# A two-layer decoder trunk on one core: x turned without its norm, the norm's factor applied behind the projections, and all attention products on 128 rows and columns

## The chip, the cores and the metric

The kernel runs on one core of a Trainium2 chip. The metric is the device time of one execution in microseconds (us), lower is better. A core has a matrix engine (TensorE, PE in the rows; PEld is its weight load), a vector engine (VectorE, DVE), a scalar engine (ScalarE, ACT) and a fourth one, GpSimd (POOL), each with its own queue that it works through in order, and queues that issue transfers (SP is the one that only does that).

## The reference, cut to what matters

```python
def rms_norm(x, g):
    y = xf * lax.rsqrt(jnp.mean(xf * xf, axis=-1, keepdims=True) + EPS)
    return (y * g.astype(jnp.float32)).astype(x.dtype)
...
    for layer in range(DEPTH):                      # DEPTH 2, x is (1, 256, 1024)
        h = rms_norm(x, norm1_g[layer])
        proj = h @ w_in[layer]
        dq, dk, dv, fq, fk, fv, ff, ga, gb = jnp.split(proj, split_points, axis=-1)
        y_diff = diff_attention(...)                # 4 heads, 2 maps of 64 each, values of 128
        y_fox = forgetting_attention(...)           # 8 heads of 64, decay from log_sigmoid(ff + b)
        merged = jax.nn.sigmoid(ga) * (y_diff @ w_diff_o[layer]) + jax.nn.sigmoid(gb) * (y_fox @ w_fox_o[layer])
        x = x + merged @ w_out[layer]
        x = x + peer_ffn(rms_norm(x, norm2_g[layer]), ...)
    return rms_norm(x, final_norm_g)

def peer_ffn(h, w_query, sub_keys, expert_u, expert_v):
    q = (t @ w_query).reshape(T, PEER_HEADS, 2, PEER_HALF)      # 8 heads
    s = jnp.einsum('thpd,pnd->thpn', q, sub_keys)
    top_s, top_i = lax.top_k(s, PEER_TOPK)                      # 16 of 128, twice; then 16 of 256
...
    gates = jax.nn.softmax(best_s, axis=-1)
...
        act = jax.nn.gelu(jnp.einsum('td,ted->te', tb, expert_u[eb]).astype(jnp.float32), approximate=False)
        return jnp.einsum('te,ted->td', (gb * act).astype(tb.dtype), expert_v[eb])   # 16384 experts
```

## The kernel before

Tokens are 256, in two halves tt of 128; the width of 1024 is eight pieces k of 128. Every large matrix product runs three times in a reduced float32 form: each operand is split into a high part (ScalarE copies it, line 92 for weights) and a low part (VectorE subtracts, line 93), and hi x hi, hi x lo and lo x hi are summed. Weights come as 656 blocks of 128 x 1024 in one fixed order (plan): per layer 8 for V and the forget gate, 32 for queries, keys and gates (wA), 8 and 8 for the output products, 16 for the expert queries (wQ), 128 for expert_u and 128 for expert_v. There are three raw buffers, filled from SP's queue, and three pairs hi and lo. A call of weights for block n first emits the splits up to block n + 2, so that the split of block n + 2 stands in ScalarE's and VectorE's queues ahead of all that is written after it, and can begin when TensorE is done with block n - 1.

The order is written by hand (manual_schedule): an instruction stands in its engine's queue where the Python code emits it, and generators such as forget, diff_head, fox_pair and select are advanced between projections by next, so that their pieces fall between the matmuls.

Per layer: norm_t makes the normalised, turned activations hT (the sums of squares on ScalarE, the root on GpSimd and VectorE, then 16 products of x with a diagonal matrix on TensorE, line 248, which norm and turn at once, then high and low parts, lines 253 and 254). mixer runs the V product (eight blocks, tokens on the rows), the projections wA with the attention heads between them, and the output products; sum_b adds the last product up, its last two blocks piece by piece in four pieces of 128 x 512, so that each piece of x is finished early. peer then has its own norm_t, 16 query projections, 48 projections of expert_u while select picks the experts on VectorE (each projection gives it 1.35 us of work, PIECE_US), then the rest of expert_u with the dense gate matrices (one_hots, dense, apply), and the sum over expert_v, again by sum_b.

## Time and profile before

| | |
|---|---|
| median of 3 runs | 2009.3 us (2009.29 to 2009.52) |
| the profiled execution | 2009.3 us, its span 2007.5 us |
| TensorE busy | 1992.8 us, 14042 matmul passes |
| VectorE, ScalarE busy | 1412.1 us, 1058.8 us |
| GpSimd busy | 27.4 us |

A busy matmul overlaps the next, so TensorE's busy time tells only that it hardly ever has nothing to do. The chain of waits is the better view: it follows the work that ended last back to what released it, and gives a matmul the time until the next one goes on. The hand-overs between the stages are the places to look at: where sum_b ends and the next projections begin.

### The profile page before, as it was taken

To read this page: it belongs to the slowest core of one execution; us is meant where nothing else is said; L and a number is where in the kernel's file an instruction comes from. 1 tells how busy PE (TensorE), PEld (TensorE's weight loads), DVE (VectorE), ACT (ScalarE), POOL (GpSimd) and SP (SyncE) were. 2 spreads that over 40 slices of the span, in tenths; PEclk is the share of its full clock that TensorE was granted. 3 is DMA by queue.
4 is the path that set the end of the run, shared out by engine and by line. 5 is a ranking of instruction groups with operands and counts; after the bars stand their busy time and mean duration, and the time that the engine had idled before them with its cause. 6 is when DMAs were issued, how large, how long until landed. Compare 5 with 4: busy or idle time off the path is not lost.

```text
span 2007.5 us, 35728 instructions
## 1 busy us (share of the span) xinstructions
PE 1992.8 (99%) x14042; PEld 1833.4 (91%) x14042; DVE 1412.1 (70%) x2867; ACT 1058.8 (53%) x1954; POOL 27.4 (1%) x49
## 2 busy tenths in 40 slices
PE   9999999999999999999999999999999999999998
PEld 8998999999999888888899989999999998888886
DVE  5667798788888555555566677987888885555555
ACT  6665556554444444444466655465444444444444
POOL 2000000000000000000010000000000000000000
PEclk9999999999999999999999999999999999999999
DMA  6445555555555555555554455565555555555554
GB/s 226 149 157 168 161 180 181 187 164 163 158 168 167 190 189 189 189 189 189 189 167 148 148 180 159 190 180 179 167 159 161 167 174 188 189 189 189 189 188 153
DMA packets 97451, 351.96 MB, mean 175 GB/s; under 512 B 11473, under 2 KB 11510, under 8 KB 97281
## 3 DMA queue, kind: packets, MB, share of 16 engines
q1 hardware_dynamic: 95040, 345.09, 54.5%
q0 software_dynamic: 1664, 3.53, 0.6%
q8 instruction: 110, 1.80, 0.4%
q10 hardware_dynamic: 576, 1.05, 0.1%
q14 instruction: 61, 0.49, 0.1%
HBM read 348.56 MB, written 1.71 MB: 174 GB/s over the span
## 4 chain that ended last, share of the span: by engine, by line
PE 99%; DVE 0%; DMA 0%; issue 0%; ACT 0%; POOL 0%; SPq 0%; ACTq 0%; DVEq 0%
PE acc L154 39%; PE ps L121 17%; PE ps L122 17%; PE ps L123 17%; PE acc L760 3%; PE ps L154 1%; PE acc L783 1%; PE acc L248 1%; PE acc L627 1%; PE ps L557 0%; PE acc L569 0%; PE acc L644 0%; DMA x<-x 0%; PE acc L122 0%; PE acc L123 0%
## 5 line engine op out<-in xcount | busy, mean ns | idle before, releaser
L93 DVE TENSOR_TENSOR lo<-raw,hi 128x1024 fp32r<-128x1024 f32 (+1 forms) x656 | 801.7, 1224 | 500.2 <-ACT hi L92 498.2
L92 ACT ACTIVATE hi<-raw 128x1024 fp32r<-128x1024 f32 (+1 forms) x656 | 694.4, 1059 | 396.3 <-PE acc L154 389.2
L121 PE MATMUL ps<-hT,hi 128*128 128x256 f32 x2784 | 794.6, 285 | 0.0
L122 PE MATMUL ps<-hT,hi 128*128 128x256 f32 x2784 | 784.6, 282 | 0.0
L123 PE MATMUL ps<-hT,lo 128*128 128x256 f32 x2784 | 778.9, 280 | 0.0
L154 PE MATMUL acc<-hi,cut 128*128 128x512 f32 x2048 | 561.1, 395 | 0.0
L121 PEld LDWEIGHTS ps<-hT,hi 128*128 128x128 f32 x2784 | 523.0, 188 | 3.9 <-issue 3.7
L123 PEld LDWEIGHTS ps<-hT,lo 128*128 128x128 f32 x2784 | 524.9, 189 | 0.0
L122 PEld LDWEIGHTS ps<-hT,hi 128*128 128x128 f32 x2784 | 523.4, 188 | 0.3
L154 PEld LDWEIGHTS acc<-hi,cut 128*128 128x128 f32 x2048 | 385.4, 188 | 90.0
L154 PE MATMUL acc<-lo,cut 128*128 128x512 f32 x1024 | 321.9, 394 | 0.0
L154 PEld LDWEIGHTS acc<-lo,cut 128*128 128x128 f32 x1024 | 192.4, 188 | 45.8
L730 ACT ACTIVATE g<-ps 128x8 f32<-128x8 f32 (+31 forms) x158 | 44.5, 282 | 265.3 <-PE ps L123 260.7
L675 ACT ACTIVATE bufa<-ps 128x256 f32<-128x256 f32 x96 | 36.9, 384 | 115.5 <-PE ps L123 115.5
L751 DVE TENSOR_TENSOR ohG<-oh,tT 128x2048 f16<-128x2048 f16 x64 | 78.4, 1225 | 2.2
L749 DVE TENSOR_TENSOR oh<-iotax,tT 128x2048 f16<-128x2048 f16 x64 | 77.8, 1216 | 0.0
L760 PE MATMUL acc<-ohG,oh 128*128 128x128 f16 x1024 | 70.0, 219 | 0.0
L701 DVE TENSOR_TENSOR cut<-bufb,cut 128x256 fp32r<-128x256 f32 x160 | 67.1, 419 | 0.0
L700 ACT ACTIVATE cut<-bufb 128x256 fp32r<-128x256 f32 x160 | 64.0, 400 | 0.0
L760 PEld LDWEIGHTS <-oh 128*128 128x128 f16 x1024 | 58.9, 97 | 2.9
L734 DVE TENSOR_TENSOR bufb<-bufb,g 128x8 f32<-128x8 f32 (+31 forms) x158 | 46.1, 292 | 15.3 <-ACT g L730 15.3
L772 DVE SCALAR_TENSOR_TENSOR bufa<-acc,bufa 128x192 f32<-128x192 f32 x128 | 44.8, 350 | 0.0
(231 smaller groups left out, 1383.9 us busy)
## 6 DMA issues: line engine op xcount, KB each, us to landing
raw<-uT SPq DMA_DIRECT2D x256, 512.0 KB, 3.7
raw<-expert_v SPq DMA_DIRECT2D x256, 512.0 KB, 3.6
raw<-wA SPq DMA_DIRECT2D x64, 512.0 KB, 3.6
raw<-wQ SPq DMA_DIRECT2D x32, 512.0 KB, 3.6
raw<-wV SPq DMA_DIRECT2D x16, 516.0 KB, 4.0
raw<-wO SPq DMA_DIRECT2D x16, 512.0 KB, 3.6
raw<-w_out SPq DMA_DIRECT2D x16, 512.0 KB, 4.4
tb<-table POOLq DMA_DIRECT2D x2, 640.0 KB, 6.1
```

Of the source, the lines that this page charges most:

```text
L92: nc.scalar.activation(hi[:, :w], raw[:, :w], AF.Copy)
L93: nc.vector.tensor_sub(lo[:, :w], raw[:, :w], hi[:, :w].bitcast(F32))
L121: self.nc.tensor.matmul(ps, ah, bh, start=first and q == 0, stop=False)
L122: self.nc.tensor.matmul(ps, ah, bl, start=False, stop=False)
L123: self.nc.tensor.matmul(ps, al, bh, start=False, stop=last and q == n - 1)
L154: self.nc.tensor.matmul(ps[:, :width], a, b[:, g * width:(g + 1) * width], start=first and n == 0, stop=last and n == 2)
L700: nc.scalar.activation(a[:, 0], chunk(n), AF.Copy)
L701: nc.vector.tensor_sub(a[:, 1], chunk(n), a[:, 0].bitcast(F32))
L734: nc.vector.tensor_mul(chunk(J)[:, :t0], chunk(J)[:, :t0], g[:, :t0])
L749: nc.vector.tensor_tensor(flat(oh), self.iotax.rearrange("p n t -> p (n t)")[:, None].to_broadcast([128, TB, 256]), cols[0][:, :, None].to ...
L751: nc.vector.tensor_tensor(flat(og), flat(oh)[:, None, TB * 128:].to_broadcast([128, 2, TB * 128]), cols[1][:, :, None].to_broadcast([128, ...
L760: self.nc.tensor.matmul(banks[t // 4][:, t % 4], oh[:, 0, t // 2, :, t % 2], og[:, k, t // 2, :, t % 2], start=k == 0, stop=k == 1)
```

## The change

x is no longer normed before it is turned. While the last pieces of sum_b still run, each finished piece of x (add) is turned by four plain transposes (tip), and ScalarE and VectorE make its high and low part with the gain (tip, turn_lo); the last piece is turned inside the next product (turn_last). V and the expert queries work on these unnormed activations: V's outputs get the factor per token when they are copied out, the expert scores in the exponential. The projections wA and uT use a scaled copy. The generator scaled makes it beside the eight V blocks, and beside the first query projections in peer: two squares on ScalarE, the root, two diagonals, a product of ones with them on TensorE, which spreads the factor over all rows (rb), and then four rounds for two k each: add, multiply, copy, subtract. In the attention the halves of the queries are kept in two tiles with zeros in the other 64 rows, so that the score products contract over 128 rows; the forget scores use 128 rows instead of 80, and the fox outputs compute 128 columns per head, of which 64 are used. At the start all of x comes over SP's queue, and the identity over ScalarE's.

```diff
-KO = [0, 2, 4, 6, 1, 3, 5, 7]
+KO = list(range(KT))
...
+    def proj_first(self, h, *key, turn=False):
...
+        if turn:
+            order = [(0, 0, lo), None, (1, 0, lo), (0, 0, up), (1, 0, up), (0, 1, KO)]
+        else:
+            order = [(0, 0, KO), (0, 1, KO), (1, 0, KO)]
+        for n, o in enumerate(order):
+            if o is None:
+                self.turn_last()
+                continue
+            for k in o[2]:
+                self.nc.tensor.matmul(ps, w[o[0]][:, k], h[o[1]][:, k], start=n == 0 and k == 0,
+                                      stop=n == len(order) - 1 and k == KT - 1)
...
+                    if last and n == 2:
+                        self.tip(2)
...
+                if turn and p == 2 and m == 0:
+                    self.tip(1)
+                    self.turn_lo(0, range(2))
             self.late.append(ps)
+            if turn:
+                if p < 3:
+                    self.add(p)
+                if p == 1:
+                    self.tip(0)
+                if p == 2:
+                    self.turn_lo(0, range(2, 4))
+                    self.turn_lo(1, range(2))
+                if p == 3:
+                    self.add(3)
+                    self.turn_lo(1, range(2, 4))
+                    self.turn_lo(2, range(4))
...
-    def norm_t(self, pool, g):
...
+    def tip(self, n):
...
+        for k in range(4):
+            nc.tensor.transpose(banks[n][:, k * 128:(k + 1) * 128],
+                                self.x[:, tt, c + k * 128:c + (k + 1) * 128], self.ident)
+        for k in range(4):
+            q = c // 128 + k
+            nc.scalar.activation(h[0][:, q, tt * 128:(tt + 1) * 128], banks[n][:, k * 128:(k + 1) * 128], AF.Copy,
+                                 scale=g[:, q:q + 1])
...
+    def turn_last(self):
+        self.tip(3)
+        self.turn_lo(3, range(4))
+
+    def scaled(self, pool, h, out, rs):
...
+            nc.scalar.activation(junk, self.x[:, tt], AF.Square, scale=1.0 / 32, accum_out=ss[:, tt:tt + 1])
+        yield
...
+        nc.tensor.matmul(ps, self.ones, diag.rearrange("p t c -> p (t c)"), start=True, stop=True)
+        rb = self.ring(pool, "rb", [128, S], F32, 1)
+        nc.scalar.activation(rb, ps, AF.Copy)
+        yield
+        for k in range(0, KT, 2):
+            t = self.ring(pool, "nt", [128, 2, S], F32, 1)
+            ks = slice(k, k + 2)
+            nc.vector.tensor_add(t, h[0][:, ks].bitcast(F32), h[1][:, ks].bitcast(F32))
+            nc.vector.tensor_tensor(t, t, rb[:, None, :].to_broadcast([128, 2, S]), op=OP.mult)
+            nc.scalar.activation(out[0][:, ks], t, AF.Copy)
+            nc.vector.tensor_sub(out[1][:, ks], t, out[0][:, ks].bitcast(F32))
+            yield
...
-                    eng = nc.scalar if tt else nc.sync
-                    eng.dma_start(self.x[:, tt, cs], i["x"][0, tt * 128:(tt + 1) * 128, cs])
+                    nc.sync.dma_start(self.x[:, tt, cs], i["x"][0, tt * 128:(tt + 1) * 128, cs])
...
-            nc.gpsimd.dma_start(self.ident, i["c_ident"])
+            nc.scalar.dma_start(self.ident, i["c_ident"])
...
-            self.norm_t(ap, self.gains[:, 0, l])
...
+            sc = self.scaled(ap, self.hT, self.hs, rs)
...
+                    if n == 0 and tt == 0:
+                        self.turn_last()
+                next(sc, None)
+                if n >= 6:
+                    next(sc, None)
...
-                nc.tensor.matmul(pss[m][:, tt * 128:tt * 256 + 128], qk[0][rows, h, tt * 128:(tt + 1) * 128],
-                                 qk[1][rows, h, 0:(tt + 1) * 128], start=True, stop=True)
+                nc.tensor.matmul(pss[m][:, tt * 128:tt * 256 + 128], dq[m][:, h, tt * 128:(tt + 1) * 128],
+                                 dk[:, h, 0:(tt + 1) * 128], start=True, stop=True)
...
-                nc.tensor.matmul(ps[:, cs], fq[n][rows, c, qs], fk[n][rows, c % 2, 0:K], start=True, stop=True)
+                nc.tensor.matmul(ps[:, cs], fq[n][:, c, qs], fk[n][:, c % 2, 0:K], start=True, stop=True)
...
-            nc.tensor.matmul(psy[o:o + 64, :], dv[:, 0, cs], wt[n][:, 0:256], start=True, stop=False)
-            nc.tensor.matmul(psy[o:o + 64, 128:256], dv[:, 1, cs], wt[n][:, 256:384], start=False, stop=True)
...
+            nc.tensor.matmul(psy[:, n], dv[:, 0, cs], wt[n][:, 0:256], start=True, stop=False)
+            nc.tensor.matmul(psy[:, n, 128:256], dv[:, 1, cs], wt[n][:, 256:384], start=False, stop=True)
...
-                    ps = self.proj("wQ", l, j + 16) if j < 0 else self.proj("uT", l, j)
+                    if j < -14:
+                        ps = self.proj_first(self.hs, "wQ", l, j + 16, turn=j == -16)
+                    else:
+                        ps = self.proj(self.hs, "wQ", l, j + 16) if j < 0 else self.proj(self.hT, "uT", l, j)
+                    if -15 <= j <= -12 or j in (-10, -8, -6, -4):
+                        next(sc, None)
...
-                    if j >= -13:
+                    if j >= -13 and j not in (-10, -8, -6, -4):
...
-        nc.scalar.activation(e, e, AF.Exp)
+            nc.scalar.activation(e[:, hs], e[:, hs], AF.Exp, scale=self.rs[1][:, tt:tt + 1])
```

The order of ScalarE's queue in the V product of layer 0, before: hi_157, hi_158 and hi_159 are the high parts of weight blocks in turn, nlam and ls belong to the attention's lambda and need a table of their own each.

```order
L92 ACTIVATE hi_159<-raw_77 128x1032
L92 ACTIVATE hi_157<-raw_75 128x1032
L92 ACTIVATE hi_158<-raw_76 128x1032
L92 ACTIVATE hi_159<-raw_77 128x1032
L386 ACT_TABLE_LOAD
L386 ACTIVATE nlam<-mhalf 128x1
L387 ACT_TABLE_LOAD
L387 ACTIVATE ls<-ls 128x2
L92 ACTIVATE hi_157<-raw_75 128x1032
L92 ACTIVATE hi_158<-raw_76 128x1032
L92 ACTIVATE hi_159<-raw_77 128x1024
L92 ACTIVATE hi_157<-raw_75 128x1024
```

And the same place now, from the split for V block 5 on (hs is the scaled copy, nt the product before it is split):

```order
L92 ACTIVATE hi_190<-raw_77 128x1032
L334 ACTIVATE rb_326<-acc_122 128x256
L488 ACT_TABLE_LOAD
L488 ACTIVATE nlam<-mhalf 128x1
L489 ACT_TABLE_LOAD
L489 ACTIVATE ls<-ls 128x2
L92 ACTIVATE hi_188<-raw_75 128x1032
L341 ACTIVATE hs_111<-nt_354 128x512
L92 ACTIVATE hi_189<-raw_76 128x1032
L341 ACTIVATE hs_111<-nt_354 128x512
L92 ACTIVATE hi_190<-raw_77 128x1024
L341 ACTIVATE hs_111<-nt_354 128x512 x2
```

The read of the ones product (rb) now stands ahead of the two table loads, and one copy of the scaling stands behind each split, two behind the third. On VectorE the order is alike: lo, then add and multiply and subtract of one round, then the next lo.

ScalarE's queue at the hand-over inside layer 0, before: the last splits of the output product, the four squares, the split of the second query block, then hT (four more rows like the last four follow, and then hi_158).

```order
L92 ACTIVATE hi_157<-raw_75 128x1024
L92 ACTIVATE hi_158<-raw_76 128x1024
L92 ACTIVATE hi_159<-raw_77 128x1024
L216 ACTIVATE hT_81,ss_115<-x 128x512 x2
L216 ACTIVATE hT_81,ss_116<-x 128x512 x2
L92 ACTIVATE hi_157<-raw_75 128x1024
L253 ACTIVATE hT_81<-acc_132,gains 128x256
L253 ACTIVATE hT_81<-acc_133,gains 128x256
L253 ACTIVATE hT_81<-acc_134,gains 128x256
L253 ACTIVATE hT_81<-acc_135,gains 128x256
```

And now: hs_111 is the high part of the turned activations, its rows are the four copies of a piece each.

```order
L92 ACTIVATE hi_188<-raw_75 128x1024
L92 ACTIVATE hi_189<-raw_76 128x1024
L92 ACTIVATE hi_190<-raw_77 128x1024
L294 ACTIVATE hs_111<-ps_88,gains 128x128 x4
L294 ACTIVATE hs_111<-ps_89,gains 128x128 x4
L294 ACTIVATE hs_111<-acc_122,gains 128x128 x4
L92 ACTIVATE hi_188<-raw_75 128x1024
L92 ACTIVATE hi_189<-raw_76 128x1024
L294 ACTIVATE hs_111<-acc_123,gains 128x128 x4
L789 ACTIVATE q_2204<-ps_90 128x256
L92 ACTIVATE hi_190<-raw_77 128x1024
L317 ACTIVATE hT_81,nss_2234<-x 128x1024 x2
```

The squares have moved behind, and the copies stand in pieces, three ahead of the splits of the next two weight blocks and the fourth behind them.

VectorE's queue at the end of the selection in layer 0, before: L938 makes the last part of tT for a half of the tokens, oh and ohG are the one-hots for the first dense product.

```order
L857 TENSOR_TENSOR rows<-prod_3509 128x128
L93 TENSOR_TENSOR lo_162<-raw_77,hi_159 128x1024
L93 TENSOR_TENSOR lo_160<-raw_75,hi_157 128x1024
L938 SCALAR_TENSOR_TENSOR tT_2065<-acc_132,tT_2065 128x16x8
L93 TENSOR_TENSOR lo_161<-raw_76,hi_158 128x1024
L938 SCALAR_TENSOR_TENSOR tT_2065<-acc_133,tT_2065 128x16x8
L93 TENSOR_TENSOR lo_162<-raw_77,hi_159 128x1024
L93 TENSOR_TENSOR lo_160<-raw_75,hi_157 128x1024
L93 TENSOR_TENSOR lo_161<-raw_76,hi_158 128x1024
L749 TENSOR_TENSOR oh_4344<-iotax,tT_2064 128x2048
L751 TENSOR_TENSOR ohG_4345<-oh_4344,tT_2065 128x2048
L93 TENSOR_TENSOR lo_162<-raw_77,hi_159 128x1024
```

And now (L1057, L866 and L868 are the same operations):

```order
L974 TENSOR_TENSOR rows<-prod_3707 128x128
L974 TENSOR_TENSOR rows<-prod_3708 128x128
L93 TENSOR_TENSOR lo_191<-raw_75,hi_188 128x1024
L93 TENSOR_TENSOR lo_192<-raw_76,hi_189 128x1024
L1057 SCALAR_TENSOR_TENSOR tT_2155<-acc_121,tT_2155 128x16x8
L1057 SCALAR_TENSOR_TENSOR tT_2155<-acc_122,tT_2155 128x16x8
L866 TENSOR_TENSOR oh_4433<-iotax,tT_2154 128x2048
L868 TENSOR_TENSOR ohG_4434<-oh_4433,tT_2155 128x2048
L93 TENSOR_TENSOR lo_193<-raw_77,hi_190 128x1024
L93 TENSOR_TENSOR lo_191<-raw_75,hi_188 128x1024
```

Three weight splits stood between the last part of tT and the one-hots, and now none. On TensorE five projections stood between the second half's transposes and the first dense product, and now one.

## Rows read from the trace of the kernel before

**Rows 1.** The page's first part: busy us, share of the span, instructions.
```profile
PE 1992.8 (99%) x14042; PEld 1833.4 (91%) x14042; DVE 1412.1 (70%) x2867; ACT 1058.8 (53%) x1954; POOL 27.4 (1%) x49
```

**Rows 2.** Chain of waits, whole run, two rows: start, length, engine, tile, line.
```profile
1012.70 1.59 PE ps L154 x10
1021.20 1.58 PE ps L154 x10
```

**Rows 3.** Chain of waits at two hand-overs: inside layer 0, and between the layers.
```profile
193.88 1.31 issue
202.40 0.12 PE ps L121
...
1002.99 1.17 PE acc L154 x5
```

**Rows 4.** Chain of waits around attention products of layer 0.
```profile
73.59 0.86 PE acc L569 x8
74.44 0.31 PE ps L121
...
80.31 0.33 PE ps L557 x3
80.64 1.31 PE acc L627 x8
...
91.80 0.59 PE acc L644 x4
92.38 0.22 PE acc L645 x4
```

**Rows 5.** Timeline at hand-overs: start, length, engine, line, operation [idle before].
```profile
1000.88 1.28 DVE L210 TENSOR_TENSOR x<-acc,x 128x512 f32<-128x512 f32 x2
...
197.94 3.27 ACT L253 ACTIVATE hT<-acc,gains 128x256 fp32r<-128x256 f32 x8 [1.64 <-PE acc L248]
198.45 3.39 DVE L254 SCALAR_TENSOR_TENSOR hT<-acc,gains,hT 128x256 fp32r<-128x256 f32 x8 [0.30 <-ACT hT L253]
```

**Rows 6.** Groups by line and shape: busy us, mean ns | idle before.
```profile
L93 DVE TENSOR_TENSOR lo<-raw,hi 128x1024 fp32r<-128x1024 f32 x640 | 782.1, 1224 | 487.4 <-ACT hi L92 485.3
L304 DVE TENSOR_TENSOR y<-x,raw 128x512 f32<-128x512 f32 x3 | 2.1, 689 | 0.1
L92 ACT ACTIVATE hi<-raw 128x1024 fp32r<-128x1024 f32 x640 | 677.3, 1059 | 384.3 <-PE acc L154 380.6 <-DMA raw<-wA 2.7 <-ACT gates L484 0.7
L484 ACT ACTIVATE gates<-gates 128x512 f32<-128x512 f32 x16 | 9.7, 619 | 0.0
```

**Rows 7.** Timeline of ScalarE in the V product of layer 1.
```profile
1019.48 1.28 ACT L386 ACT_TABLE_LOAD   x1
...
1022.40 1.05 ACT L92 ACTIVATE hi<-raw 128x1032 fp32r<-128x1032 f32 x1
```

**Rows 8.** Timeline of ScalarE and VectorE at the end of the selection, layer 0.
```profile
380.19 0.38 ACT L675 ACTIVATE bufa<-ps 128x256 f32<-128x256 f32 x1 [1.34 <-PE ps L123]
380.47 0.44 ACT L933 ACTIVATE tT<-acc 128x128 f16<-128x128 f32 x2
380.79 0.30 ACT L937 ACTIVATE tT<-acc 128x128 f16<-128x128 f32 x1
...
388.35 1.22 DVE L749 TENSOR_TENSOR oh<-iotax,tT 128x2048 f16<-128x2048 f16 x1
389.60 1.23 DVE L751 TENSOR_TENSOR ohG<-oh,tT 128x2048 f16<-128x2048 f16 x1
```

**Rows 9.** The start: timeline of TensorE, an issued transfer, POOL's clearing.
```profile
11.75 0.71 PE L154 MATMUL ps<-hi,hT 128*128 128x344 f32 x3
15.53 0.64 PE L154 MATMUL ps<-hi,hT 128*128 128x344 f32 x3
...
gains<-norm_g POOLq DMA_DIRECT2D x1, 16.0 KB, 5.7
L399 POOL MEMSET fq<- 64x1024 f32 x2 | 1.9, 973 | 0.0
```

154 lines of the change are left out of this document (99 added, 55 removed).

## The prediction

> **What bounds the kernel now.** The page first: TensorE is busy 1992.8 of 2007.5 us, VectorE 1412.1, ScalarE 1058.8 [rows 1]. So only two things change the time: what TensorE executes, and what makes it wait. Hence the chain of waits, in order of time. Outside the hand-overs between stages it is an unbroken row of matmuls: in the V product three blocks lie between 1012.70 and 1021.20, so each takes 2.83 us [rows 2]. At a hand-over it breaks. In the middle of layer 0 the output product ends at 193.88, the second query block starts at 202.40; its first block is 2.83 us of matmuls, so the hand-over costs 8.52 - 2.83 = 5.7 us, of which 1.31 is waiting and most of the rest the 32 passes of the norm's turn (L248) [rows 3]. Between the layers it is the same: end at 1002.99 + 1.17 = 1004.16, second V block at 1012.70, again 8.54 us in all [rows 2, 3]. The start has such a turn too. The three hand-overs are 17 us together, under 1% of the time, so little can be won, and a new wait of a few us per layer outweighs it.
>
> **The change, part by part.**
>
> *Attention products.* The chain shows each kind as a block. Four score products of a diff head (64 rows, x8 passes) take 0.86 us, and the next matmul 0.31 where 0.12 is normal: 1.05 us. The fox scores (80 and 128 rows, same columns) take 1.31. The fox output (64 columns) takes 0.59 + 0.22, and with the same 0.19 behind it 1.00 [rows 4]. After the change diff scores have exactly the shape of the fox scores with 128 rows, and the fox output issues the same passes (four of 256 and four of 128 columns) on a full array, so both cost 1.31. There are 4 heads and 4 pairs per layer, 8 of each: 8 x 0.26 + 8 x 0.31 = **+4.6 us**. In the fox scores half of the products have 128 rows already, and I take the same 1.31 when all have. Bounds: 0, if the full shape ran like the split one, and +5.2, if the 0.19 after a block stayed too in half of the cases. The blocks already run two products side by side: the 64-row block holds as many passes as the fox block and is shorter. [...]
>
> *Hand-over between the layers.* Gone are the 5.7 us. Added: 16 transposes of 0.33/3 = 0.11 us [rows 4], 1.8 us, three quarters of them inside the tail of the sum; and a wait before the first. That one needs x after the first add, and this add stands on VectorE behind the split of the next weight block: the two adds ran from 1000.88 for 1.28 us [rows 5], so the first is done at 1001.52, while TensorE is free at 1001.2: 0.45 us with the signal. The rest is in time: the V product's first half needs only pieces done by then. 8.54 - (1.76 + 0.45 + 2.83) = **-3.5 us**.
>
> *Hand-over inside a layer, twice.* Same work on TensorE, but the query product needs all 256 tokens at once, thus pieces 2 and 3. ScalarE's order (shown above) is four copies of piece 2, two weight splits, four copies of piece 3. A copy with gain took 3.27/8 = 0.41 at 256 columns, so 0.30 at 128 (less 128 at 0.86 ns, the slope between its 512 and 1024 rows); VectorE's partner 3.39/8, so 0.29; a split 1.06 and 1.23 [rows 5, 6]. From the end of the sum: with tail transposes T = +1.76; the first four matmuls wait for copies until +2.77; piece 3's transposes are done at +3.21, but its copies stand behind the two splits and finish at +5.8; VectorE's low parts stand behind lo, lo and finish at +7.87; block 0 ends at +8.1 where it ended at +8.5. So **-0.45 us each**, -0.9, and not -3.5: the two splits are what is late next.
>
> *The norm itself.* Each of four times a product of ones and the diagonals: 256 columns in float32, two passes of about 0.22: 4 x 0.43 = **+1.7 us**. Its VectorE operand is ready a block earlier.
>
> *The V product, where scaling runs beside it.* This is the big term. Per pair of k the scaling is add, multiply (VectorE, 128x512), copy (ScalarE), subtract (VectorE), each waiting for the one before. Rows: 0.69 for a VectorE operation of that size (about 0.6 where another follows, as with the two adds [rows 5]), 0.62 for the copy [rows 6]. In the order above it lies between the splits on both engines. So the splits no longer go side by side with it: split 7's hi waits behind the copy, the copy waits for the multiply, the multiply stands behind lo 6. One round is lo 1.15, add 0.62, multiply 0.69, copy 0.62, hi 1.06 with small overlaps: **4.1 us against 2.83 of matmuls**. Nor does it begin with a lead. The Ln and Exp loads stood behind split 5 and took 2.92 us (1019.48 to 1022.40) [rows 7]; now they stand behind the read of the ones product, which comes only after block 3. Counting from the end of block 3 (0.43 for that product): read done +1.02, loads until +3.94, hi 6 until +5.0, lo 6 until +6.26, wanted at +6.58. Before, hi 6 began at 1022.40, 1.2 after the same point. Then: hi 7 ready +9.12, lo 7 +10.38, where block 7 wants them at +8.95 and +9.42: 1.0 us lost, block 7 ends +12.8. Split 8, first of the projections, is ready at +14.5, 1.45 more; its k 4 and 5 exist at +17.1, k 6 and 7 at +19.7, since the last two rounds follow one another. The first projection ends at +20.35 instead of +14.63: 5.7 us. Split 9 then stands behind those copies, 0.7 more. Split 11 is in time again, because scores stand before the fourth projection. So 6.4 us per layer, **+12.8 us**. Bounds: 0, if the splits ran far enough ahead, and 9 per layer, if the forget gate's Ln and Exp also come late. I take the walk.
>
> *End of the selection, twice.* Four of the steps that advance it now serve the scaling, so it ends about four blocks later: its last transposes stand right before the last projection ahead of the first dense product, where five projections stood between. ScalarE then needs 0.38 for the gelu and 2 x 0.47 for turned rows, VectorE 0.29 as above, and the one-hots 2.48 [rows 8]: 4.3 us after the 47th block, and TensorE gets there after 0.33 + 2.83 = 3.2. **+1.2 each, +2.4.** Bounds 0 and 2.4 each (if a split comes between). Scaling itself is covered there: a query block with its score is 3.3 us and splits stand two blocks ahead.
>
> *Start.* Before: V's first block starts at 11.75, and the second at 15.53 [rows 9]. Now x needs no norm first, but every copy needs the gains, issued from POOL's queue and 5.7 us under way: about 7.0. Twelve copies of 0.30 and then the first split's 1.07 make 11.7 for the start; lo 0 and a fourth turn make 15.8 for the second block: +0.3, bounds -2 and +1.5 by the landing of the gains. The two lower pieces of x change to SP's queue, ahead of the weights, and the identity to ScalarE's; both land before the gains, so neither is on this path. POOL clears six halves per layer instead of two, under 1 us each, while the first projections run; without that cover the first scores would wait some 4 us.
>
> Sum: 4.6 - 3.5 - 0.9 + 1.7 + 12.8 + 2.4 + 0.3 = +17.4. The profiled execution took 2009.3 us (span 2007.5 and 1.8 around it), the median of the runs is 2009.3 as well: **2026.7 us**.
>
> **Rivals.**
>
> *V covered.* The scaling hides in V as it does in the query product. For it: before, VectorE and ScalarE have idle time there, and a split may run two blocks ahead. Against: the loads eat that lead, and the round of 4.1 is a chain, not a load. Without the 12.8: 2013.9.
>
> *TensorE's own balance alone, the one that ends faster.* One mechanism: ScalarE's and VectorE's queues never reach TensorE, so every wait of V, query hand-over and selection falls away. Then 4.6 - 3 x 3.5 + 1.7 + 0.3 = -3.9: 2005.4. It decides where a V round falls under 2.83 us or the splits start a block earlier, which no row shows. Switching between split and full arrays could add to it only what lies around the 16 blocks, 0.19 behind each, 3.0 us, and that is in the 1.05 and 1.00 already. [...]
>
> *Worse.* The lateness stays into the first attention heads, where ScalarE now copies the queries in halves, or the raws are fetched late behind late splits: 3 to 5 us more per layer, about 2036.
>
> **How the numbers follow.** Forecast 0.58 (its own range 2020 to 2032), V covered 0.17 (2010 to 2018), TensorE alone 0.15 (2002 to 2009), worse 0.10. The range 2007 to 2033 leaves out most of the third and the upper half of the last. About 0.2% (4.0 us) is what a measurement of this kernel can tell from no change. Under 2005.3 lies most of the third case: 0.13. Between, its rest and the lower end of the second: 0.12. Slower: 0.75.
>
> **What would show it.** The chain of waits should leave TensorE between the fourth V block and the second projection, in both layers, naming lo (L93) and hs (L342) as releasers, 5 to 7 us each. Diff scores and fox outputs should be blocks of 1.31. Query block 0 should wait for hs behind two splits and end about 8.1 us after the sum's old end. The first dense product should wait some 1.2 us for the one-hots. Wrong it would be if V's blocks keep their 2.83 us through to the projections; then the sum is 2014 at most, and less if the query hand-over waits are absent too.

## The result, and the profile after

The changed kernel takes **2040.75 us** (median of 5 runs, 2039.61 to 2041.89), the kernel before 2009.31 (5 runs, 2009.29 to 2009.52): ratio 1.0157, 95% interval 1.0145 to 1.0169. It is slower, as forecast, but by 31.4 us where the forecast had 17.4, and above the range's upper end of 2033. The profiled execution has a span of 2039.0 us against 2007.5, so its difference of 31.45 can be taken apart.

TensorE's row of the page, which answers to [rows 1]: it has 14 us more of busy time, with 56 matmul passes fewer.

```profile
PE 2007.0 (98%) x13986; PEld 1845.5 (91%) x13986; DVE 1450.4 (71%) x2951; ACT 1079.1 (53%) x2008; POOL 32.9 (2%) x52
```

Next TensorE's waits, grouped by the instruction that waits and the one that ends the wait: us in total, times, the longest.

```profile
PE acc L172 <- ACT hi L92: 4.9, 3, 4.6
PE acc L121 <- ACT hs L341: 3.0, 4, 1.3
PE acc L900 <- ACT q L789: 3.0, 4, 1.0
PE ps L146 <- ACT hs L294: 2.2, 4, 0.9
PE acc L877 <- DVE ohG L868: 2.1, 2, 1.1
PE acc L123 <- DVE lo L93: 1.5, 2, 0.8
PE acc L332 <- DVE diag L329: 1.4, 1, 1.4
...
PE ps L290 <- DVE x L277: 0.7, 3, 0.2
```

Each line is a place: the first weights (L172 from hi, 4.6 at once at the start), the end of V (hs L341, lo L93), the query scores (L900), the hand-over inside a layer (L146), the end of the selection (L877), the ones product (L332), the first transpose of each hand-over (L290). The waits alone don't say what each costs. For that I read the start times of the same matmul in both traces, from one stage to the next; the difference grows or shrinks where time is lost or won.

| from ... to | start before, after | later by | this stage | forecast |
|---|---|---|---|---|
| start to second V block, layer 0 | 15.53, 20.14 | 4.61 | **+4.61** | +0.3 |
| to the forget gate's product (V's end, 3 projections) | 44.81, 58.00 | 13.19 | **+8.58** | +6.8 |
| to the output sum (attention) | 171.44, 186.91 | 15.47 | +2.28 | +2.3 |
| to the first score (hand-over) | 205.07, 219.76 | 14.69 | -0.78 | -0.45 |
| to the 13th score (query phase) | 244.46, 261.70 | 17.24 | **+2.55** | +0.43 |
| to the first dense product (selection) | 391.31, 409.90 | 18.59 | +1.35 | +1.2 |
| to the second V block, layer 1 | 1012.53, 1027.62 | 15.09 | -3.50 | -3.5 |
| to the forget gate's product | 1040.88, 1065.64 | 24.76 | **+9.67** | +6.8 |
| to the output sum | 1167.48, 1194.52 | 27.04 | +2.28 | +2.3 |
| to the first score | 1201.09, 1227.46 | 26.37 | -0.67 | -0.45 |
| to the 13th score | 1240.47, 1269.43 | 28.96 | **+2.59** | +0.43 |
| to the first dense product | 1387.38, 1417.61 | 30.23 | +1.27 | +1.2 |
| to the last matmul, then the end | 1999.85, 2030.06; span 2007.53, 2038.98 | 30.21; 31.45 | +1.22 | 0 |

The 6.8 of V are the walk's 6.4 and one ones product, the 0.43 of the query phase another. Four things are off and make up the missing 14: the start 4.3, V's end 4.6 in both layers, the query phase 4.3, the end 1.2, less 0.5 at the hand-overs.

TensorE's granted clock is the second view. Before, it was full (1.00) from 4.26 us, where its records begin, to 2004.47, behind the last matmul. After, it falls to half (0.50) three times in between: from 12.89 for 6.83 us, from 47.02 for 6.83, from 1057.37 for 3.41. The row gives a stretch, then busy time of PE, PEld, DVE, ACT and POOL, the clock as a share of full, the DMA share and GB/s. Ahead of each stretch TensorE had waited: for the first weights (9.3 to 13.9 us), and in the first attention projection.

```profile
12.90:19.70 6.80, 5.77 (x20) 5.27 (x21) 4.09 (x5) 4.63 (x8) 0.00 (x0) 0.50 0.61 185
47.00:53.80 6.80, 5.95 (x24) 5.36 (x25) 5.55 (x11) 4.61 (x9) 0.00 (x0) 0.50 0.24 71
1057.40:1060.80 3.40, 3.23 (x14) 2.94 (x15) 3.08 (x4) 3.40 (x6) 0.00 (x0) 0.50 0.09 13
```

### The profile page after: what moved, and what is told of

Its sections match the earlier page's. It is cut to its first block, busy times and chain, and to the rows that moved or that the text cites. A ratio compares the mean times of both kernels' runs of the same rounds, so it can differ in the third digit from the quotient of the medians.

```text
span 2039.0 us, 35731 instructions
## 1 busy us (share of the span) xinstructions
PE 2007.0 (98%) x13986; PEld 1845.5 (91%) x13986; DVE 1450.4 (71%) x2951; ACT 1079.1 (53%) x2008; POOL 32.9 (2%) x52
## 5 line engine op out<-in xcount | busy, mean ns | idle before, releaser
L93 DVE TENSOR_TENSOR lo<-raw,hi 128x1024 fp32r<-128x1024 f32 (+1 forms) x656 | 801.2, 1223 | 482.6 <-ACT hi L92 479.9
L121 PE MATMUL ps<-hT,hi 128*128 128x256 f32 x2048 | 580.8, 284 | 0.0
L122 PE MATMUL ps<-hT,hi 128*128 128x256 f32 x2048 | 576.7, 282 | 0.0
L123 PE MATMUL ps<-hT,lo 128*128 128x256 f32 x2048 | 573.0, 280 | 0.0
L172 PE MATMUL acc<-hi,cut 128*128 128x512 f32 x2016 | 551.1, 395 | 0.0
L172 PEld LDWEIGHTS acc<-hi,cut 128*128 128x128 f32 x2016 | 379.4, 188 | 88.6
L123 PEld LDWEIGHTS ps<-hT,lo 128*128 128x128 f32 x2048 | 386.1, 189 | 0.0
L122 PEld LDWEIGHTS ps<-hT,hi 128*128 128x128 f32 x2048 | 384.8, 188 | 0.0
L121 PEld LDWEIGHTS ps<-hT,hi 128*128 128x128 f32 x2048 | 384.6, 188 | 0.0
L172 PE MATMUL acc<-lo,cut 128*128 128x512 f32 x1008 | 315.6, 394 | 0.0
L172 PEld LDWEIGHTS acc<-lo,cut 128*128 128x128 f32 x1008 | 189.5, 188 | 45.1
L121 PE MATMUL ps<-hs,hi 128*128 128x256 f32 x704 | 205.4, 292 | 0.0
L122 PE MATMUL ps<-hs,hi 128*128 128x256 f32 x704 | 198.2, 282 | 0.0
L123 PE MATMUL ps<-hs,lo 128*128 128x256 f32 x704 | 197.1, 280 | 0.0
L122 PEld LDWEIGHTS ps<-hs,hi 128*128 128x128 f32 x704 | 132.5, 188 | 0.4
L121 PEld LDWEIGHTS ps<-hs,hi 128*128 128x128 f32 x704 | 132.4, 188 | 0.4
L123 PEld LDWEIGHTS ps<-hs,lo 128*128 128x128 f32 x704 | 132.8, 189 | 0.0
L868 DVE TENSOR_TENSOR ohG<-oh,tT 128x2048 f16<-128x2048 f16 x64 | 78.4, 1225 | 2.2
L866 DVE TENSOR_TENSOR oh<-iotax,tT 128x2048 f16<-128x2048 f16 x64 | 77.6, 1212 | 0.0
```

The source lines that it names most:

```text
L93: nc.vector.tensor_sub(lo[:, :w], raw[:, :w], hi[:, :w].bitcast(F32))
L121: self.nc.tensor.matmul(ps, ah, bh, start=first and q == 0, stop=False)
L122: self.nc.tensor.matmul(ps, ah, bl, start=False, stop=False)
L123: self.nc.tensor.matmul(ps, al, bh, start=False, stop=last and q == n - 1)
L172: self.nc.tensor.matmul(ps[:, :width], a, b[:, g * width:(g + 1) * width], start=first and n == 0, stop=last and n == 2)
L866: nc.vector.tensor_tensor(flat(oh), self.iotax.rearrange("p n t -> p (n t)")[:, None].to_broadcast([128, TB, 256]), cols[0][:, :, None].to ...
```

## The experiments

Each is compared with the kernel before, run beside it (2009.3 to 2009.5); "change" is against the changed kernel's 2040.75, whose own runs spread over 2.3 us, so a change under 1 us tells nothing by itself.

| run | us | change | ratio to before, 95% interval |
|---|---|---|---|
| e1_attention | 2014.21 | | 1.0022 (1.0012 to 1.0032) |
| e2_norm | 2034.11 | -6.6 | 1.0122 (1.0105 to 1.0139) |
| e3_no_rounds | 2019.14 | -21.6 | 1.0046 (1.0030 to 1.0063) |
| e4_start | 2039.35 | -1.4 | 1.0148 (1.0131 to 1.0165) |
| e5_skew | 2033.28 | -7.5 | 1.0117 (1.0100 to 1.0134) |
| e6_loads | 2036.07 | -4.7 | 1.0128 (1.0112 to 1.0145) |
| e7_fill | 2039.24 | -1.5 | 1.0146 (1.0129 to 1.0163) |
| e8_select | 2037.98 | -2.8 | 1.0139 (1.0122 to 1.0156) |
| e9_evict | 2025.24 | -15.5 | 1.0079 (1.0062 to 1.0096) |
| e10_best | 2009.29 | | 1.0000 (0.9991 to 1.0010) |
| e11_clears | 2038.23 | -2.5 | 1.0142 (1.0125 to 1.0159) |
| e12_startfill | 2040.93 | +0.2 | 1.0155 (1.0138 to 1.0172) |
| e13_startfill28 | 2040.33 | -0.4 | 1.0153 (1.0137 to 1.0168) |
| e14_best2 | 2007.63 | | 0.9992 (0.9983 to 1.0001) |
| e15_order | 2038.50 | -2.3 | 1.0145 (1.0129 to 1.0160) |
| e16_best3 | 2007.18 | | 0.9990 (0.9981 to 0.9999) |
| e17_best4 | 2023.94 | | 1.0074 (1.0060 to 1.0088) |
| e18_best5 | 2006.40 | | 0.9985 (0.9976 to 0.9994) |

**The two halves of the change: e1_attention, e2_norm.** The first is the kernel before with the hunks of diff_head and fox_pair and the copies in halves and clears that belong to them, the second the changed kernel without them.

> The kernel before with the full-array attention products alone; norm and turn as before. The prediction's term: 8 diff scores and 8 fox outputs at 1.31 us instead of 1.05 and 1.00, +4.6, so 2013.9. By the profile after (offsets of the two kernels at the first score and at the output sum) +2.4 per layer, 2014.0. [...] Rival, that the copies in halves hold up ScalarE in the attention heads: over 2016.

> The changed kernel with the attention products of before; the turn without norm and the scaling stay. If the two changes add up: 2040.8 - 4.7 = 2036.0. If the split array costs more beside the new waits, or less, it lies outside 2034.5 to 2037.5.

Alone, the attention products cost 4.67 us, as forecast. The blocks can be read in the changed kernel: start, length, engine, line, shape, count.

```profile
87.17 1.47 PE L679 MATMUL acc<-dk,dq 128*128 128x128 f32 x8
88.29 0.47 PE L121 MATMUL ps<-hs,hi 128*128 128x256 f32 x1
88.59 0.28 PE L122 MATMUL ps<-hs,hi 128*128 128x256 f32 x1
...
105.61 0.59 PE L753 MATMUL acc<-wt,dv 128*128 128x256 f32 x2
...
106.83 0.36 PE L121 MATMUL ps<-hs,hi 128*128 128x256 f32 x1
107.03 0.28 PE L122 MATMUL ps<-hs,hi 128*128 128x256 f32 x1
```

From the block's start to that of the next matmul 88.29 - 87.17 = 1.12, and that one takes 0.30 where 0.12 is normal [rows 3]: 1.30 for the scores, and 1.22 + 0.08 = 1.30 for the fox outputs, against 1.05 and 1.00 [rows 4]. The timeline before shows where the 1.05 lay: the block starts 0.21 behind the matmul ahead of it, where 0.12 is normal, takes 0.86, and the next matmul 0.21.

```profile
73.31 0.28 PE L123 MATMUL ps<-hT,lo 128*128 128x256 f32 x1
73.52 0.93 PE L569 MATMUL acc<-dk,dq 64*128 64x128 f32 x8
74.38 0.38 PE L121 MATMUL ps<-hT,hi 128*128 128x256 f32 x1
74.59 0.28 PE L122 MATMUL ps<-hT,hi 128*128 128x256 f32 x1
```

So 0.18 us lie around a score block on either array, half of it ahead on the split one and all of it behind on the full one; around the fox outputs it is 0.08 on the full array and 0.19 on the split one. What of it, if any, comes from switching between split and full arrays is not shown; what is shown is that the full array costs more in all (4.67). Without these products the changed kernel falls by 6.6, 2.0 more than they cost alone and outside the bounds I had set: the two parts don't just add. By the stages of the table 1.2 of it lie in the start and 0.5 in V of layer 0, where half clock lasts 3.41 us each time instead of 6.83, and 0.8 in the end; V of layer 1 takes 0.4 more. None of these is an attention product.

**Is it the scaling rounds? e3_no_rounds.** The four lines of the round in scaled are left out:

```diff
-                        ps = self.proj(self.hs, "wA", l, 4 * q + c, tag="acc" if c == 0 and q < 2 else "ps")
+                        ps = self.proj(self.hT, "wA", l, 4 * q + c, tag="acc" if c == 0 and q < 2 else "ps")
```

> The changed kernel with all the rounds of the scaling left out (add, multiply, copy, subtract), in V and in the query phase; attention reads the turned input without its factor and the uT projections read an old tile, so only the time means something. The factor itself, the ones product and the Ln and Exp loads stay. Theory, that the rounds' chain is what TensorE waits for: V loses about 5.7 us of waits per layer and the half clock behind them (3.4 and 1.7), the query phase 2.1 per layer, together -20: about 2021. Rival, that late weight splits from the turn itself and the loads are the cause: the projections still wait, and it falls by less than 8, over 2033.

It falls by 21.6. For this and the next runs the stages of the table, as they stand against the kernel before:

| us more than before | V's end, layer 0 | layer 1 | query phase, layer 0 | layer 1 |
|---|---|---|---|---|
| changed kernel | 8.58 | 9.67 | 2.55 | 2.59 |
| e3_no_rounds | 0.43 | 2.06 | 0.43 | 0.40 |
| e5_skew | 7.38 | 8.47 | 0.43 | 0.42 |
| e6_loads | 5.50 | 8.23 | 2.56 | 2.57 |
| e7_fill | 7.45 | 9.14 | 2.57 | 2.60 |
| e11_clears | 8.49 | 8.64 | 2.57 | 2.58 |
| e13_startfill28 | 9.48 | 10.14 | 2.56 | 2.59 |
| e18_best5 | 0.42 | 0.42 | 0.43 | 0.40 |

Without rounds 0.43 is left, the ones product, and in layer 1 another 1.6, to which e11_clears comes. So the rounds, with the half clock that follows their waits, cost 8.2 and 7.6 in V and 2.1 in each query phase; the rest of the 21.6 lies in the start and in the end.

**How the round waits: e5_skew, e6_loads.** The timeline of the changed kernel in V of layer 1, ScalarE's rows first, then VectorE's:

```profile
1038.40 0.38 ACT L334 ACTIVATE rb<-acc 128x256 f32<-128x256 f32 x1 [3.64 <-PE acc L332]
1038.79 1.28 ACT L488 ACT_TABLE_LOAD   x1
...
1041.70 1.05 ACT L92 ACTIVATE hi<-raw 128x1032 fp32r<-128x1032 f32 x1
1045.38 0.63 ACT L341 ACTIVATE hs<-nt 128x512 fp32r<-128x512 f32 x1 [2.63 <-DVE nt L340]
1045.92 1.05 ACT L92 ACTIVATE hi<-raw 128x1032 fp32r<-128x1032 f32 x1
...
1042.79 1.23 DVE L93 TENSOR_TENSOR lo<-raw,hi 128x1032 fp32r<-128x1032 f32 x1 [3.69 <-ACT hi L92]
1043.94 0.68 DVE L339 TENSOR_TENSOR nt<-hT,hT 128x512 f32<-128x512 f32 x1
1044.66 0.69 DVE L340 TENSOR_TENSOR nt<-nt,rb 128x512 f32<-128x512 f32 x1
1046.05 0.69 DVE L342 TENSOR_TENSOR hs<-nt,hs 128x512 fp32r<-128x512 f32 x1 [0.70 <-ACT hs L341]
```

hi at 1041.70, the next at 1045.92: a round is 4.22 us (4.1 in the walk), and in it each engine waits for the other. The two loads stand behind the read of rb, as the order had it, and the first split behind them begins 3.3 us after that read. e5_skew splits the round over two steps of the generator (half is the copy and the subtract), and e6_loads moves lambda's two activations from n == 3 to n == 2:

```diff
+            if k:
+                half(k - 2, t)
             nc.vector.tensor_add(t, h[0][:, ks].bitcast(F32), h[1][:, ks].bitcast(F32))
             nc.vector.tensor_tensor(t, t, rb[:, None, :].to_broadcast([128, 2, S]), op=OP.mult)
-            nc.scalar.activation(out[0][:, ks], t, AF.Copy)
-            nc.vector.tensor_sub(out[1][:, ks], t, out[0][:, ks].bitcast(F32))
             yield
```

> The changed kernel with each scaling round cut in two: add and multiply at one step, copy and subtract at the next, so that ScalarE's copy no longer stands in its queue waiting for a multiply that VectorE has yet to reach. Theory, that the round is a chain through two engines (4.2 us from hi to hi in the profile after): what is left is VectorE's own 1.2 + 0.7 + 0.7 + 0.6 = 3.2 per round; V loses about 3 us per layer and some of the half clock, and the waits of the query phase go (2.1 per layer): -10 to -15, 2026 to 2031. Rival, that VectorE's load and not the order bounds both places: V unchanged, the query phase down by 1 at most per layer, 2037 to 2041.

> The changed kernel with the Ln and Exp of lambda (each with its table load, 3 us together on ScalarE) one V block earlier, ahead of the read of the ones product instead of behind it. The prediction's walk has the loads delay split 6 and all rounds behind it by 2.9 us: -2.9 per layer, with some of the half clock -6 to -9, 2032 to 2035. Rival, that the first round waits for something else (the ones product itself, or VectorE): within 1 us of the changed kernel.

e5_skew as run also leaves out the last copy and subtract of each query phase. Its query phases have no wait left (-2.1 each, as the theory said), but V wins only 1.2 per layer instead of 3: with the round cut, VectorE works in layer 1 from 1038.59 to 1053.5 with one break of 0.7, so its load takes over from the order. The truth lies between theory and rival: order in the query phase, order and then load in V. e6_loads wins 3.1 in layer 0, where half clock lasts 3.41 us instead of 6.83 as well, and 1.4 in layer 1, where the ones product is late itself: the loads count, as the walk had it, but for 4.7 in all and not the 6 to 9 expected.

**The half clock in V: e7_fill.**

```diff
+        self.fill(4)
+            for n, (a, b) in enumerate(pair):
+                self.fill({(0, 2): 7, (4, 0): 6, (4, 1): 5, (6, 0): 8, (6, 1): 5}.get((k, n), 0))
```

> The changed kernel with 35 filler matmuls per layer (256 columns into a spare bank, 0.12 us each) in the first attention projection, in front of the six matmuls that wait for a split or a scaled part, so many as fit into each wait. They do no useful work. Theory, that the half clock after these waits (6.8 and 3.4 us in the profile after) costs time by itself: the clock stays full there, and the sum falls by 2.4 + 1.7 = 4, to 2036.7. Rival, that the matmuls at half rate only fill time that would be waited anyway, or that the clock falls for another reason: no change, or up to 2 us more.

The clock stays full from 19.57 us to the end, and V's end takes 1.1 and 0.5 us less: 1.7 of the 4 expected (1.13 and 0.53). Most of what half rate adds falls into time in which the projection waited for the next scaled part anyway.

**The late ones product: e11_clears.** In layer 1 the ones product waits 1.4 us for the diagonals, in layer 0 not at all. VectorE's rows in both layers, then GpSimd's:

```profile
26.01 0.17 DVE L326 TENSOR_SCALAR rs<-rs_y 128x2 f32<-128x2 f32 x1
26.21 0.48 DVE L329 TENSOR_SCALAR diag<-ident,rs 128x128 f32<-128x128 f32 x2
...
1035.10 1.40 DVE L326 TENSOR_SCALAR rs<-rs_y 128x2 f32<-128x2 f32 x1
1036.54 1.07 DVE L329 TENSOR_SCALAR diag<-ident,rs 128x128 f32<-128x128 f32 x2
1037.53 1.22 DVE L93 TENSOR_TENSOR lo<-raw,hi 128x1032 fp32r<-128x1032 f32 x1
...
1035.07 0.95 POOL L504 MEMSET fq<- 64x1024 f32 x1
1035.96 0.52 POOL L505 MEMSET fk<- 64x512 f32 x1
1036.51 0.94 POOL L504 MEMSET fq<- 64x1024 f32 x1
```

An operation on two numbers per partition takes 1.40 us where it took 0.17, and ends just when the first two clears end. The edit puts the clears behind the diagonals by one small copy on GpSimd that reads them:

```diff
+            nc.gpsimd.tensor_copy(after, self.diag[:, 1, 0:1])
             for o in range(2):
                 free = slice(64 - o * 64, 128 - o * 64)
```

> The changed kernel with GpSimd's six clears of half tiles behind a copy of one element per partition of the diagonals, so that in layer 1 they start only when the factor and the diagonals are done. Theory, that VectorE's operation on 128x2 took 1.40 us in layer 1 (0.17 in layer 0) and the two diagonals 1.07 (0.48) because the clears ran beside them: both fall back, the ones product of layer 1 waits 1.4 less, and with it the rounds: -1.4, 2039.4. Rival, that the factor waits for something else there: unchanged.

The same two rows then, and the ones product no longer waits:

```profile
1034.27 0.17 DVE L326 TENSOR_SCALAR rs<-rs_y 128x2 f32<-128x2 f32 x1
1034.47 0.48 DVE L329 TENSOR_SCALAR diag<-ident,rs 128x128 f32<-128x128 f32 x2
```

V's end of layer 1 falls by 1.0, though its half clock is longer in this run (6.83 us). Of the 2.5 in all, 0.7 stand ahead of V's first block, where the edit does nothing. e2_norm tells whose clears these are. It has only the two per layer that the kernel before has too, and they stand beside the small operation all the same; only the diagonals are free of them there, and the ones product waits 0.8 us.

```profile
1031.09 1.38 DVE L326 TENSOR_SCALAR rs<-rs_y 128x2 f32<-128x2 f32 x1
1032.51 0.48 DVE L329 TENSOR_SCALAR diag<-ident,rs 128x128 f32<-128x128 f32 x2
```

So GpSimd's clears held up the norm's part: 0.8 us with two of them, 1.4 with the four that the attention part added.

**Scaling at the eviction: e9_evict.** Here V has no rounds, and VectorE multiplies where ScalarE copied a projection out.

```diff
-                        nc.scalar.activation(gates[:, 4 * c + q - 4], ps, AF.Copy)
+                        nc.vector.tensor_mul(gates[:, 4 * c + q - 4], ps, self.rb)
```

> The changed kernel without scaling rounds in V: the attention projections read the turned input as it is, and VectorE multiplies each projection by the factor (read of the ones product) where ScalarE copied it out. The query phase keeps its rounds. Theory, that the rounds are what V's end waits for: V's end costs little more than the ones product and its wait, as in the kernel without rounds (8.5 and 7.6 less per layer), and VectorE's 13 to 18 us more per layer in the attention heads lie beside TensorE: 2024.7. Rival, that these evictions make VectorE late there (scores, splits): over 2028.

2025.24, near the theory's 2024.7; the rival shows up as one wait of 0.7 and 0.2 us for fk in each layer's first head, and the attention stage takes 3.45 and 2.80 us more than before instead of 2.28.

**End of the selection: e8_select.**

```diff
-                        debt += PIECE_US
+                        debt += PIECE_US * (1.12 if j >= 0 else 1.0)
```

> The changed kernel with 12% more selection work per uT projection, which makes up for the four steps given to the scaling, so that the selection ends as early as before. Theory: the first dense product no longer waits for the one-hots, 1.3 per layer: -2.5, 2038.2. Rival, that VectorE then is late for the weight splits between: no change or slower.

-2.8, and TensorE no longer waits before the first dense products.

**The query hand-over: e15_order.**

```diff
+        if turn:
+            self.limit = self.used + 1
...
                 self.turn_last()
+                self.limit = limit
+                self.ahead(self.used + 2)
```

> The changed kernel with one change at the hand-over inside a layer: the two weight splits that stand on ScalarE and VectorE between the third and the fourth turn's copies come behind the fourth. The prediction has these splits as what is late next there. Theory: the wait before the upper parts (1.13) goes, -1.0 per layer, 2038.7. Rival, that the splits are then late for the second block by as much: 2040 to 2041.

-2.3. In the rows of the changed kernel the copies of the last turn stand behind two splits, and the upper half of the first query block waits for them; after the edit the first block takes 4.64 us instead of 5.79, and the second is not late.

```profile
214.28 1.16 PE L146 MATMUL ps<-hs,hi 128*128 128x256 f32 x4 [0.86 <-ACT hs L294]
...
211.94 2.02 ACT L92 ACTIVATE hi<-raw 128x1024 fp32r<-128x1024 f32 x2
213.84 1.16 ACT L294 ACTIVATE hs<-acc,gains 128x128 fp32r<-128x128 f32 x4
```

**The start: e4_start, e12_startfill, e13_startfill28.** The third turn waited for its piece of x, V's first block for its split, and the split for its load; the last row is the weight loads of the first 13 us: count, KB, median us from issue to landing.

```profile
8.61 0.66 PE L290 MATMUL acc<-ident,x 128*128 128x128 f32 x4 [0.90 <-DMA x<-x]
...
12.77 1.06 ACT L92 ACTIVATE hi<-raw 128x1032 fp32r<-128x1032 f32 x1 [2.26 <-DMA raw<-wV]
...
raw<-wV SPq DMA_DIRECT2D x3, 516.0 KB, 11.6
```

Before, these loads took 6.0 us. e4_start gives the lower half of x back to ScalarE's queue; the other two put fillers in TensorE's wait.

```diff
-                    nc.sync.dma_start(self.x[:, tt, cs], i["x"][0, tt * 128:(tt + 1) * 128, cs])
+                    eng = nc.scalar if tt else nc.sync
+                    eng.dma_start(self.x[:, tt, cs], i["x"][0, tt * 128:(tt + 1) * 128, cs])
...
+                for _ in range(12):
+                    nc.tensor.matmul(self.turning[2][3][:, 0:128], self.ones, self.ones, start=True, stop=True)
```

> The changed kernel with the lower two pieces of x on ScalarE's queue again, behind the identity; nothing else moves. Theory, that the first weight block lands late because all of x stands ahead of it on SP's queue: V's first block starts at about 11.5 instead of 13.9 us, and TensorE's clock, which fell to half from 12.9 to 19.7 us, stays full or falls for less; -2 without the clock, -4.5 with it, 2036.3 to 2038.8. Rival, that the many small loads of POOL's queue hold the weights: no change within 1 us.

> The changed kernel with 12 filler matmuls (128 columns of float32) between the first three turns and V's first block, in TensorE's wait for the first weights. Theory, that the half clock from 12.9 to 19.7 us follows that wait and costs 2.4 us of V's first block (6.41 us long): the clock stays full and the sum falls by about 2, to 2038.7. Rival, that the first block waits for its low parts and the fourth turn anyway: within 0.7.

> The changed kernel with 28 filler matmuls before V's first block instead of 12, 6.0 us of TensorE work in its wait of about 5.5. With 12 they ended 3.4 us before V began and the clock fell all the same. Theory, that the half clock at the start follows the wait and costs about 2 us of V's first block (6.4 us long, 4.0 before): the clock stays full, the block takes 4 to 4.5 us, 2038.5. Rival, that the block waits for its low parts and the fourth turn: the clock is full, the block as long as it was, 2040 to 2041.

With e4_start V begins at 11.63 instead of 13.89 us, so x ahead of the weights on SP's queue is the cause of that. The next two weight blocks still land at 12.15 and 13.63 us (8.80 and 10.05 before); GpSimd's further loads, issued from 1.9 us on and before from 8.8, were not tried as a cause. The clock falls all the same (11.18 to 18.01), of the 2.3 won 1.8 are left at the second block, and the median falls by 1.4, less than the 2 to 4.5 expected. The 12 fillers ended 3.1 us before V began and changed nothing. With 28 the clock is full, and the first block takes 4.20 us instead of 6.41: 1.9 won there. But V's end then takes 0.9 more. The rounds come 1.9 earlier as well (the last matmul that waits for a scaled part starts at 47.99 instead of 49.87), but the clock falls at 47.15, about when it did in the changed kernel (47.02). So 6.0 us at half clock lie behind that wait instead of 4.0, on matmuls that have nothing left to wait for and start every 0.21 us instead of 0.12. The medians show little (-0.4).

**All parts together: e10_best, e14_best2, e16_best3 to e18_best5.** They keep the turn without norm, with attention products as before, e9_evict, e5_skew with its last half round, e4_start with 12 fillers, e8_select and e11_clears; e14_best2 adds e15_order and more fillers, and the last three move VectorE's half of the split in sum_b's tail:

```diff
-            nc.vector.tensor_sub(lo[:, :w], raw[:, :w], hi[:, :w].bitcast(F32))
+                self.later.append((lo[:, :w], raw[:, :w], hi[:, :w].bitcast(F32)))
...
                 if p < 3:
                     self.add(p)
+                if p == 0:
+                    for args in self.later:
+                        self.nc.vector.tensor_sub(*args)
```

> All that the runs point to together: the turn without norm, attention products of before, the factor at the eviction of the attention projections, rounds of the query phase cut in two (with the last copy and subtract in place), x on two queues with 12 filler matmuls before V, clears of GpSimd behind the diagonals, 12% more selection work per uT projection. By the sum of the parts: start +0.5 to +1, the last turn 0.44, ones products 4 x 0.43, between the layers -3.4, inside a layer -0.7 twice, so -1 to -2 against the kernel before: about 2008. Rival, that VectorE's evictions wait or the start is not mended: 2010 to 2014.

> The version of all parts once more (2009.3, level with the kernel before), with 17 fillers before V's first block and 6 in it before its low parts, and with the fourth turn's copies of the query hand-over ahead of the weight splits. By the parts: -2 for the start if its clock stays full, -1 for each hand-over inside a layer: 2005.3, 0.2% under the kernel before. Rival, that the later splits make the second query blocks wait as long, and that the start's clock falls again: 2009.

> The last version of all parts, with one more change at the three hand-overs: VectorE's half of the split that stands ahead of the first add in the tail of each sum comes behind that add. In all kernels so far the first transpose waits 0.6 us there for x. Theory: the add is then done when TensorE gets to the transposes, -0.5 three times, 2006.1, with the interval against the kernel before wholly under 1. Rival, that the low part is then late for the next stage's first block or the later adds slip: 2007.6 or more.

> The last version of all parts, now with VectorE's half of the split that stands ahead of the first add of each hand-over really behind it (one block further back than in the run before, whose edit moved no instruction). Theory, from the prediction: the first transpose waits because the add stands behind this split, 0.4 us each time (0.63 from matmul to transpose where 0.23 is normal): -1.2, 2006.2. Rival, that the split's half is then late for the next stage, or that the signal alone takes the time: 2007.4 as the same program had twice.

> As the run before, but the load into the raw buffer that the moved half still reads is issued behind that half too. In the run before it was issued ahead of it, so VectorE's half waited for that load (3.6 us at the first hand-over) and split other data than meant. Theory: with the load in its place the first transpose no longer waits, -0.4 three times, 2006.2. Rival: the signal from VectorE takes the time, or the later load makes the next stage wait: 2007.4 or more.

e10_best is level with the kernel before and not under it (2008 expected): in its profiled execution (2011.06 us) V's first block, at half clock, takes 6.24 us. e14_best2 is 1.75 us under it (2005.3 expected), with an interval that just reaches 1; its clock is full from 5.9 us on. The edit of e16_best3 was one step too late and moved no instruction: the same program again, 2.2 under. In e17_best4 the moved half of the split waited for a load at each hand-over, so it tells nothing of the question:

```profile
197.00 1.23 DVE L223 TENSOR_TENSOR lo<-raw,hi 128x1024 fp32r<-128x1024 f32 x1 [3.60 <-DMA raw<-wQ]
```

e18_best5 has the order that was meant. The waits for x at the transposes (L290 in the changed kernel) are gone, and it takes 2006.40 (2006.2 expected), 2.9 us under the kernel before. Its list of waits is short:

```profile
PE acc L764 <- DVE fk L567: 1.1, 2, 0.9
PE ps L403 <- DVE ones L400: 1.1, 1, 1.1
PE ps L154 <- ACT hs L311: 0.4, 2, 0.2
```

## Why the prediction was right in direction and too small

The forecast was 14 us short. Three of its terms failed: V with its ones products (13.7 forecast, 18.25 measured), the query phase, where scaling was called covered (0 forecast beside the ones products, 4.3 measured), and the start (+0.3, measured +4.61). The end (+1.2) had no term.

**Right, and of the right size.** The attention products (4.6 forecast, 4.56 in the table, 4.67 alone). The hand-over between the layers (-3.5, measured -3.50). The selection (2.4, measured 2.62, and e8_select takes it away). The hand-over inside a layer was better than forecast, -1.45 instead of -0.9 for both, and its reason held: e15_order shows that the two splits are what was late next. The half of the split ahead of the first add was a wait, too, as the step said (e18_best5).

**The V product: mechanism right, term too small.** "This is the big term" was right: a chain through two engines, 4.22 us per round (walk 4.1), the table loads ahead of it (e6_loads), lo and hs as releasers. But 12.8 + 0.86 was forecast and 18.25 came. Two things are shown for the missing 4.6. The step "its VectorE operand is ready a block earlier" failed in layer 1: the clears on GpSimd, which I priced at nothing because the projections hide them from TensorE, held up VectorE, and TensorE waited 1.4 us for the diagonals; e11_clears wins 1.0 of it. Two of these clears are as old as the kernel before; on the new path to the factor they cost 0.8 by themselves (e2_norm). And the half clock after the waits, which no step had, cost 1.7 (e7_fill). The remaining 1.5 I didn't separate.

**"Scaling itself is covered there" failed.** The query phase lost 2.1 per layer beside the ones product. I compared the length of a query block with a split two blocks ahead, and left out the selection, which stands on VectorE between the same operations. The rows show the consequence, VectorE's first: selection (L910 is its first operation of several, up to 243.9), split, then the round's multiply at 245.66; ScalarE's copy of the round waits for it, the copy of q stands behind that, and the score waits for q.

```profile
241.47 0.48 DVE L910 MAX8 tv<-s 128x8 f32<-128x128 f32 x2
...
243.82 1.21 DVE L93 TENSOR_TENSOR lo<-raw,hi 128x1024 fp32r<-128x1024 f32 x1
...
245.66 0.69 DVE L340 TENSOR_TENSOR nt<-nt,rb 128x512 f32<-128x512 f32 x1
...
246.39 0.63 ACT L341 ACTIVATE hT<-nt 128x512 fp32r<-128x512 f32 x1 [4.25 <-DVE nt L340]
...
247.19 0.38 ACT L789 ACTIVATE q<-ps 128x256 f32<-128x256 f32 x1
...
247.61 0.71 PE L900 MATMUL acc<-sk,q 128*128 128x128 f32 x4 [1.00 <-ACT q L789]
```

e5_skew cuts the round in two and the waits go; with the last half round, which it leaves out, in place they stay away too (e10_best: 0.43 and 0.41). It was the order in the queues, not VectorE's load.

**The start (+0.3, measured +4.61).** I followed the gains and wrote that the moved pieces of x "land before the gains, so neither is on this path". They don't: the gains land at 4.60 us, sooner than the 7.0 forecast, and the two moved pieces at 8.57 and 11.46. The weights queue behind them, and these I left where they were before, so the first lands at 12.75 instead of 7.63: 2.1 us later for V's first block, which e4_start wins back. Another 2.5 is that block at half clock, 6.41 us instead of 3.95 (11.75 [rows 9] to 15.70); 1.9 of it goes when the clock is kept up (e13_startfill28).

**The end (+1.2)** was in no step. From the last matmul to the end it is 7.68 us before and 8.92 after; over all runs it takes one of three values, 7.7, 8.1 and 8.9. It is 8.1 in e2_norm, e3_no_rounds, e5_skew and e9_evict, so 0.8 us of what each of these wins lies here. What sets it was not tried.

**The rivals.** "Worse", 2036, came nearest, but its mechanism didn't occur: the attention heads lose their forecast 2.3 and no more, and ScalarE's splits wait for no load there. "TensorE's own balance alone", 2005.4, asked that ScalarE's and VectorE's queues never reach TensorE. Its 0.13 under 2005.3 was too much for a sum of 2005.4 with a range of 2002 to 2009. e18_best5 is near that state in V and the query phase (the ones products alone are left). Without the attention products' 4.6 that balance gives 2000.8; it stops 5.6 short, since a hand-over inside a layer still waits for the copies, the first head of each layer for fk, and the start is 1.1 us later than before.

## What to carry to other kernels

Where work moves beside an engine that has time left by its busy share, write out the queues of both helper engines for one period, with everything that already stands in them: a copy that waits in order holds up what stands behind it (ScalarE's copy of the query round waited 4.25 us here, and TensorE's score 1.00 for the q behind that copy), and cutting the round into two steps took that wait away (e5_skew and e10_best, 2.1 us per query phase). Moving a transfer to another queue has to be priced for what stands behind it there (here the first weights, which landed at 12.75 us instead of 7.63), and an operation "hidden" from one engine for what it does to the others (GpSimd's clears, beside which VectorE's 0.17 us became 1.40). A wait that TensorE did not have before can cost more than its length: here the matmuls behind it ran at half clock, starting every 0.21 us instead of 0.12, and most of that was hidden only where they would have waited anyway (1.7 us of V's cost went when e7_fill kept the clock full).

## What the runs showed of the hardware that I had not expected

VectorE's small operation beside GpSimd's clears: 0.17 us alone, 1.40 beside two clears that follow one another, 0.95 and 0.52 us long (1.38 beside the two of e2_norm), while a subtraction of two 128x1032 operands beside the next clears took its normal 1.22. The small operation ended at 1036.50 and the second clear at 1036.48, so the wait went on through two instructions. Why the one was held up and the other not is not shown.

Half clock cost far less than half where the matmuls waited anyway: in V of layer 0 it lasted 6.83 us and cost 1.1 (e7_fill), in layer 1 3.41 and 0.5. In e13_startfill28 6.0 of the same 6.83 us lay behind the last wait instead of 4.0, and V's end took 0.9 more. And how long it lasts differs between the profiled executions of nearly the same program in V of layer 1: 3.41 us in the changed kernel, 6.83 with e8_select, e11_clears and e13_startfill28.
